# A 4 KB store of zeros into the output, issued behind the first loads

## Chip, cores, metric

One core of a Trainium2 chip. The time is device microseconds of one execution; the median of several is quoted. Kernels are compared only within the same rounds.

## The reference

A 3x3 convolution with padding 1, `x` of 16 x 64 x 64 x 64 and a weight of 128 x 64 x 3 x 3 in float32, nine tenths of the weight zero. The output is 16 x 128 x 64 x 64 in float32, 33.55 MB.

```
for b, co, ci, kh, kw:
    if weight[co, ci, kh, kw] != 0:
        output[b, co] += weight[co, ci, kh, kw] * x_pad[b, ci, kh:kh+h, kw:kw+w]
```

## The kernel before

Images are worked in eight pairs (64 channels of each image on one half of the partitions). GpSimd's queue loads x and casts it to bf16 on the way; SyncE's queue loads the weights and the head of the first pair in float32, and later stores the results, one image (2 MB) at a time, the last pair in four pieces of 1 MB. TensorE is kept warm with 27 matmuls on zeros until data is there.

```
    xs = [x_pool.tile([128, H, W], BF16, name=f"x{p}") for p in range(NP)]
    w_sb = const_pool.tile([C_OUT, C_IN * KH * KW], FP32, name="w_sb")
    nc.sync.dma_start(out=w_sb, in_=weight.rearrange("o i kh kw -> o (i kh kw)"))
    x_head = o_pool.tile([128, H, W], FP32, name="o")
    nc.sync.dma_start(out=x_head[:, 0:HEAD, :], in_=pair(0)[:, 0:HEAD, :])
    nc.gpsimd.dma_start(out=xs[0][:, HEAD:H, :], in_=pair(0)[:, HEAD:H, :])
    ...
    for p in range(1, NP):
        nc.gpsimd.dma_start(out=xs[p], in_=pair(p))

    idle_rhs = const_pool.tile([128, 128], BF16, name="idle_rhs")
    nc.vector.memset(idle_rhs, 0.0)
    idle_ps = psum_pool.tile([128, 128], FP32, name="ps")
    for _ in range(27):
        nc.tensor.matmul(idle_ps, idle_rhs, idle_rhs, start=True, stop=True)
    ... (weights cast and transposed, products, additions)
    for p in range(NP):
        o = [o_pool.tile([C_OUT, H, W], FP32, name="o") for _ in range(2)]
        last = p == NP - 1
        for blk in range(4):
            ... (16 rows of both images)
            if last and blk % 2 == 1:
                for n in range(2):
                    rows = slice(r0 - 16, r0 + 16)
                    nc.sync.dma_start(out=out[2 * p + n][:, rows, :], in_=o[n][:, rows, :])
        if not last:
            for n in range(2):
                nc.sync.dma_start(out=out[2 * p + n], in_=o[n])
```

Of the kernel before, what the change touches and what calls it, by code (L numbers as in the profile page):

```python
# [8 lines left out]
FP32 = mybir.dt.float32  # L9
# [18 lines left out]
def kernel(  # L28
# [6 lines left out]
    nc = tc.nc  # L35

    B, C_IN, H, W = x.shape
# [5 lines left out]
    const_pool = ctx.enter_context(tc.tile_pool(name="const", bufs=1))  # L43
# [25 lines left out]

    idle_rhs = const_pool.tile([128, 128], BF16, name="idle_rhs")  # L70
    nc.vector.memset(idle_rhs, 0.0)  # L71
    idle_ps = psum_pool.tile([128, 128], FP32, name="ps")
    for _ in range(27):
        nc.tensor.matmul(idle_ps, idle_rhs, idle_rhs, start=True, stop=True)  # L74
# [144 lines left out]
```

## Time and profile before

| | before |
|---|---|
| time, first 3 runs | 127.72 us (127.55 to 127.75) |
| span of the profiled run (which took 127.12 us, less than the three above) | 125.4 us |
| TensorE busy from / last addition ends | 7.12 / 111.76 us |
| first store issued / its first packet | 21.60 / 25.76 us |
| last landing that SyncE waits for | 124.2 us |

From the page of the kernel before: the busy tenths of the DMA engines in 40 slices, the packet counts, SyncE's queue (packets, MB, share of 16 engines' time), and the stores (KB each, median us from issue to landing).

```profile
DMA  5999999989999999999999999999999999999980
...
DMA packets 4044, 42.93 MB, mean 342 GB/s; under 512 B 448, under 2 KB 448, under 8 KB 704
...
q1 hardware_dynamic: 2880, 34.90, 66.2%
...
out_dram<-o SPq DMA_DIRECT2D x14, 2048.0 KB, 19.8
```

The DMA engines are full from the second slice nearly to the last, and a store of 2 MB takes 19.8 us to land, four times the 4.9 us that its bytes need at 428 GB/s. Stores queue up: the kernel is bound by DMA engine time, although TensorE is busy for most of the span too. (While x is loaded the rate is only some 220 GB/s with the engines just as full: the 7.86 MB that the page gives for GpSimd's queue are half of the 15.7 MB of float32 that it reads, so its bytes are counted after the cast.)

### The profile page before, as it was taken

The page shows a single profiled execution, that of the slowest core. Times are in us where ns is not written, and L with a number is a line of the kernel's source. Part 1 is how long each engine was busy: PE and PEld are TensorE (multiplying, and loading weights), DVE is VectorE, ACT ScalarE, POOL GpSimd, SP SyncE. Part 2 cuts the span into 40 slices and gives each one's busy share as a digit, 9 for nine tenths or more (in the row PEclk, how much of TensorE's full clock was granted, in tenths as well). Part 3 has the DMA queues.
Part 4 walks back from the last instruction along what each step waited for, and adds up shares of the span by engine and source line. Part 5 has one row for each costly group of instructions (what it writes and reads, how often), then busy time and mean ns, then how long its engine had stood idle before and what let it go on. Part 6 is the DMA issues. An engine that isn't in the chain of part 4 may idle for free.

```text
span 125.4 us, 2486 instructions
## 1 busy us (share of the span) xinstructions
PE 107.5 (86%) x1002; PEld 58.8 (47%) x1002; DVE 82.4 (66%) x135; ACT 39.0 (31%) x71; POOL 40.7 (32%) x45
## 2 busy tenths in 40 slices
PE   6679999999999999999999999999999999920000
PEld 6435555555555555555555555555555555500000
DVE  0463877877787778777877787778777877760000
ACT  4555323333333333333333333333333333300000
POOL 6936533333333333333333333333333300000000
PEclk9999999999999999999999999999999999997555
DMA  5999999989999999999999999999999999999980
GB/s 146 338 222 220 212 214 220 191 259 350 324 311 337 308 293 319 342 316 308 426 429 423 408 429 434 450 416 434 418 418 429 429 444 423 434 397 423 423 369 10
DMA packets 4044, 42.93 MB, mean 342 GB/s; under 512 B 448, under 2 KB 448, under 8 KB 704
## 3 DMA queue, kind: packets, MB, share of 16 engines
q1 hardware_dynamic: 2880, 34.90, 66.2%
q0 software_dynamic: 1152, 7.86, 30.7%
q8 instruction: 8, 0.13, 0.4%
q14 instruction: 4, 0.03, 0.1%
HBM read 17.07 MB, written 33.55 MB: 404 GB/s over the span
## 4 chain that ended last, share of the span: by engine, by line
PE 81%; DMA 4%; DVE 1%; issue 1%; DVEq 0%; SPq 0%
PE ps L135 81%; DMA o<-in_x_dram 4%; DVE o L168 1%; DVEq L214 0%; DVE x L87 0%; SPq L60 0%; DVEq L168 0%
## 5 line engine op out<-in xcount | busy, mean ns | idle before, releaser
L168 DVE TENSOR_TENSOR o<-ps,pc 128x512 f32<-128x512 f32 x124 | 77.8, 686 | 22.1 <-PE ps L135 19.8
L135 PE MATMUL ps<-x,wT 64*128 64x504 bf16 (+3 forms) x780 | 88.8, 373 | 1.5 <-DVE x L87 1.5
L135 PEld LDWEIGHTS <-wT 64*128 64x128 bf16 x966 | 55.2, 94 | 49.4 <-issue 1.5
L154 POOL TENSOR_TENSOR s<-x 128x512 bf16<-128x512 bf16 x31 | 35.6, 1152 | 57.7 <-PE ps L135 41.5
L161 ACT COPY pc<-ps 128x512 f32<-128x512 f32 x62 | 33.3, 589 | 64.0 <-issue 61.8
L135 PE MATMUL ps<-s,wT 64*128 64x512 bf16 (+1 forms) x186 | 25.7, 377 | 0.0
L74 PE MATMUL ps<-idle_rhs 128*128 128x128 bf16 x27 | 3.1, 310 | 1.0 <-DVE idle_rhs L71 1.0
L67 POOL DMA_DIRECT2D x<-in_x_dram x7 | 3.7, 561 | 0.0
L74 PEld LDWEIGHTS <-idle_rhs 128*128 128x128 bf16 x27 | 2.8, 144 | 1.0 <-DVE idle_rhs L71 1.0
L91 DVE CAST w_bf<-w_sb 128x192 bf16<-128x192 f32 (+1 forms) x4 | 1.3, 382 | 3.0 <-DMA w_sb<-in_weight_dram 3.0
L149 DVE COPY o<-ps 128x512 f32<-128x512 f32 x2 | 1.4, 692 | 2.0 <-PE ps L135 2.0
L148 ACT COPY o<-ps 128x512 f32<-128x512 f32 x2 | 1.2, 586 | 2.4 <-PE ps L135 2.4
L87 ACT CAST x<-o 128x576 bf16<-128x576 f32 (+1 forms) x2 | 1.5, 802 | 0.5 <-DMA o<-in_x_dram 0.5
L91 ACT ACT_TABLE_LOAD x1 | 1.3, 1283 | 0.7 <-PEq L203 0.7
L97 PE MATMUL ps<-ident,w_bf 128*128 128x128 bf16 x9 | 1.1, 292 | 0.4 <-DVE w_bf L91 0.4
L87 DVE CAST x<-o 128x576 bf16<-128x576 f32 x1 | 0.5, 460 | 1.4 <-DMA o<-in_x_dram 1.4
L91 ACT CAST w_bf<-w_sb 128x64 bf16<-128x64 f32 (+1 forms) x2 | 0.7, 418 | 1.9 <-DMA w_sb<-in_weight_dram 1.9
L97 PEld LDWEIGHTS <-w_bf 128*128 128x128 bf16 x9 | 0.8, 128 | 0.8 <-DVE w_bf L91 0.8
L101 DVE TENSOR_TENSOR wT<-ps,wT 128x384 bf16<-128x384 f32 x2 | 1.0, 550 | 0.0
L63 POOL DMA_DIRECT2D x<-in_x_dram x1 | 0.7, 696 | 0.8 <-POOLq L203 0.8
L71 DVE MEMSET idle_rhs<- 128x64 uint32 x1 | 0.1, 112 | 0.8 <-PEq L203 0.8
L110 ACT CAST wT<-ps 128x384 bf16<-128x384 f32 x1 | 0.5, 481 | 0.4 <-PE ps L97 0.4
(8 smaller groups left out, 1.9 us busy)
## 6 DMA issues: line engine op xcount, KB each, us to landing
out_dram<-o SPq DMA_DIRECT2D x14, 2048.0 KB, 19.8
x<-in_x_dram POOLq DMA_DIRECT2D x7, 1024.0 KB, 29.3
out_dram<-o SPq DMA_DIRECT2D x4, 1024.0 KB, 12.3
o<-in_x_dram SPq DMA_DIRECT2D x1, 1024.0 KB, 5.4
x<-in_x_dram POOLq DMA_DIRECT2D x1, 512.0 KB, 7.5
w_sb<-in_weight_dram SPq DMA_DIRECT2D x1, 288.0 KB, 3.1
```

Source lines behind the costliest of these rows:

```text
L67: nc.gpsimd.dma_start(out=xs[p], in_=pair(p))
L74: nc.tensor.matmul(idle_ps, idle_rhs, idle_rhs, start=True, stop=True)
L87: copy(out=xs[0][:, a:b, :], in_=x_head[:, a:b, :])
L91: copy(out=w_bf4[:, g, a:b, :], in_=w_v[:, k : k + b - a, :])
L97: nc.tensor.matmul(wps[:, j, :], src, ident, start=True, stop=True)
L101: nc.vector.tensor_tensor(out=wT[:, g], in0=wps, in1=wT[:, G1], op=SUB)
L135: nc.tensor.matmul(ps[n][:, lo:hi, c_lo:c_hi], tap(g, kw, n), src[q, a:b:step, c_lo + kw - 1 : c_hi + kw - 1], start=(i == 0), stop=(i == ...
L148: nc.scalar.copy(out=o[0][:, r0 : r0 + rows, :], in_=ps[0])
L149: nc.vector.tensor_copy(out=o[1][:, r0 : r0 + rows, :], in_=ps[1])
L154: nc.gpsimd.tensor_tensor(out=s, in0=xs[p][:, r0 : r0 + 16 : 2, :], in1=xs[p][:, r0 + 1 : r0 + 16 : 2, :], op=ADD)
L161: nc.scalar.copy(out=c, in_=shared[n])
L168: nc.vector.tensor_tensor(out=o[n][:, first : r0 + 16 : 2, :], in0=ps[n], in1=pc[n], op=ADD)
```

## The change

Each of the 16 DMA engines makes one small write to the output early, while compute waits for its first data. The intent isn't written down; the likely one is to have whatever the first write to the output costs out of the way before the real stores begin. The real store of image 0 overwrites the rows.

```
     nc.vector.memset(idle_rhs, 0.0)
+
+    zeros = const_pool.tile([16, W], FP32, name="zeros")
+    nc.vector.memset(zeros, 0.0)
+    nc.sync.dma_start(out=out[0, 0:16, 0, :], in_=zeros)
     idle_ps = psum_pool.tile([128, 128], FP32, name="ps")
```

## The prediction

> **What bounds the kernel now.** I read the chain of waits first, then distrusted it. It follows compute and ends with DVE:
>
> ```profile
> 1.17 5.41 DMA o<-in_x_dram
> ...
> 7.12 102.09 PE ps L135 x954
> ...
> 111.16 0.60 DVE o L168
> ```
>
> The columns are start in us, length in us, and what ran. TensorE is busy without a hole from 7.12 to 109.21, but the last addition is over at 111.76 and the span is 125.4 us. The chain says nothing of the last 13.6 us, in which only stores land. So the second view is what the store queue waited for:
>
> ```profile
> SPq L188 <- DVE o L168: 92.2, 14, 19.9
> SPq L214 <- DMA out_dram<-o: 11.6, 4, 4.4
> ```
>
> SyncE waits for results all through the kernel (92.2 us in 14 waits) and at the end for four landings (11.6 us). That the tail takes so long is a backlog of the DMA engines, and the third view, the run cut into stretches, shows it. The last two numbers of each line are the share of time the 16 DMA engines are busy and the GB/s they move:
>
> ```profile
> 2.00:3.00 1.00, 1.00 (x13) 1.00 (x11) 0.00 (x0) 0.02 (x1) 0.93 (x3) 1.00 1.11 345
> ...
> 7.00:20.00 13.00, 12.88 (x120) 6.83 (x121) 8.25 (x15) 5.52 (x10) 6.82 (x6) 1.00 1.04 217
> 20.00:22.00 2.00, 2.00 (x22) 1.14 (x20) 2.00 (x4) 0.54 (x2) 0.43 (x1) 1.00 1.09 229
> 22.00:23.00 1.00, 1.00 (x14) 0.57 (x10) 0.40 (x2) 0.54 (x2) 0.71 (x1) 1.00 0.96 197
> 23.00:24.00 1.00, 1.00 (x14) 0.50 (x10) 1.00 (x3) 0.00 (x0) 0.00 (x0) 1.00 1.17 213
> 24.00:25.00 1.00, 1.00 (x12) 0.53 (x10) 1.00 (x2) 0.37 (x1) 0.28 (x1) 1.00 1.25 164
> 25.00:26.00 1.00, 1.00 (x12) 0.56 (x10) 0.27 (x2) 0.70 (x2) 0.87 (x1) 1.00 0.73 156
> 26.00:62.00 36.00, 36.00 (x342) 19.28 (x339) 28.42 (x46) 11.83 (x22) 12.69 (x11) 1.00 1.02 326
> 62.00:110.00 48.00, 48.00 (x452) 25.67 (x450) 37.54 (x61) 16.12 (x30) 13.84 (x12) 1.00 1.01 428
> 110.00:121.00 11.00, 0.40 (x6) 0.00 (x0) 1.76 (x3) 0.00 (x0) 0.00 (x0) 0.71 1.00 421
> ```
>
> The engines are full from 2 us to 121 us (a packet is counted where it starts, hence shares over 1). The end is therefore set by DMA work: the start near 2 us, plus all bytes at the rate they go, plus the last landing. Compute only has to hand over stores before the backlog runs dry. How near that is: the 13th store is issued at 98.38, and the 12th (issued 86.17, 18.1 us to landing) lands at 104.3, so 5.9 us of slack at the tightest of the late places I worked out. A delay of TensorE of under some 5 us costs nothing in the end time; DMA engine time costs its full length.
>
> One oddity carries the uncertainty. At 22 to 26 us the rate falls below the 229 GB/s of the two microseconds before: missing are 32 + 16 + 65 + 73 = 186 GB/s over one microsecond each, that is 0.186 MB, or 0.81 us of the engines at 229 GB/s. In the single packets of the trace, loads of 8 KB that always take 0.624 us take 0.7 to 1.4 us between 23.4 and 26.6 us. The excess is 0.74 us per engine. The first store is issued just before, at 21.60, and its first packet starts at 25.76. No later store shows such a dip. I read it as a start-up cost of the first write to HBM, which is argued from timing only. The change looks meant for this: one small early write from each of the 16 engines.
>
> **What the Trainium skill says.** "DMA: Bandwidth & Descriptors", section "Why a DMA increments its semaphore by 16 and not by 1": the number of engines is the largest up to 16 that divides the slowest dimension, so 16 partitions give one row of 256 B per engine. The trace of before has no such transfer; it does have 128 data packets and 16 semaphore packets for each transfer (2880 packets on the hardware queue are 20 times 144). The same page, "Queues, rings and completion order": each engine takes one queue's descriptors in ring order. The trace agrees: the first packet of the head of x starts at 2.553 us, as the weights' last ones drain. The same page, "Specifications", has transfers under 512 B done as a read-modify-write; no packet of data that small is in this trace. "Trace Analysis", section "Roofline": a lone core is bounded by its 16 engines at about 435 GB/s in aggregate, not by its HBM share. The trace agrees, 428 GB/s from 62 to 110 us.
>
> **The change, part by part.** I compared the instruction order and semaphores of both builds. TensorE, ScalarE and GpSimd have the same instructions with the same waits.
>
> VectorE: one more memset of 64 words per partition, next to that of idle_rhs. That one has the same length per partition and took 0.112 us, ending at 0.93. The next VectorE work waits for the weights until 3.91, so 0.11 us goes into 2.97 us of idle. TensorE's warm-up waits only on the first memset. Nothing.
>
> SyncE: one more issue after the second load, whose 0.42 us ends at 1.59. Like its neighbours it takes 0.33 to 0.42 us and ends near 2.0; the next issue is at 21.60. Nothing.
>
> DMA work: per engine one data packet of 256 B and one semaphore packet. The trace gives semaphore packets 9 to 22 ns, and the smallest data packets, 2304 B, 93 ns typically. I take up to 0.09 us for the data, more than its bytes need, which leaves room for a read-modify-write. Sum: 0.01 + 0.09 = up to 0.1 us on a path that is full, so +0.05 to +0.1 us at the end. As bytes alone it would be 4 KB at 428 GB/s, 0.01 us.
>
> Where they fall: on the same ring behind the head of x, whose last data packet starts at 5.67 us. So the zeros move near 6 us and land near 7 to 8 us. The head's landing, which releases TensorE, isn't behind them.
>
> Waits: the first real store overwrites these rows and now waits for the zeros' landing too. That is done more than 10 us before its other waits end at 21.60, so it adds nothing. The semaphores of SyncE's DMAs rotate over eight; the extra DMA moves every store by one place, but a store that waits for a store still waits for the one eight before it. The renamed waits on VectorE mean the same.
>
> SBUF: 256 B more per partition, which shifts the later buffers. I expect nothing of it.
>
> Sum without the oddity: 127.72 + 0.1 = 127.8 us.
>
> **Rivals.** First, the start-up cost is paid by the zeros and is hidden, because a write of 256 B holds no large data back while loads keep streaming. Then the dip at 22 to 26 us goes, and the end comes 0.74 to 0.81 us earlier: about 127.0. For it: the dip occurs once, at the first write, and the new store touches each engine. Against it: in before the dip stretched packets of the loads, so whatever waits blocks them too.
>
> Second, the cost is paid once but not hidden: it moves to some time between 3 and 7 us, where the engines are just as full. The end stays, 127.7 to 127.8. It might push the landing of the head of x and so TensorE's start from 7.12 to as late as 7.9, which the slack of 5.9 us absorbs. A reader of the chain of waits alone would expect that to cost 0.8 us; I don't.
>
> Third, the cost is not tied to the first write but to large stores joining the loads, or to new addresses in the output. The zeros warm only 16 rows of the first image. Then the dip stays at 22 to 26 us: 127.7 to 127.8. If the zeros bring their own start-up cost besides, it is paid twice, 128.5.
>
> A fourth, that the new wait on the first store delays the stores, would need the zeros to land after 21.6 us. They would have to sit behind the loads' queue, which has its own ring, so I give it next to nothing.
>
> **Range and chances.** I give 55% to no net effect (127.7 to 127.8, rivals two and three), 30% to some or all of the gain (127.0 to 127.5), 15% to a second cost (up to 128.5). The three runs of before span 0.2 us. The middle of that is 127.6, with 126.9 to 128.2 for 8 in 10. 2% is 2.55 us; the largest cost or gain I can point at is 0.8 us, so both outer outcomes get 2%.
>
> **What would show it.** In the changed profile: the hardware queue has 2912 packets and 480 lie under 512 B (448 before); a 4 KB issue from zeros by SyncE starts near 1.6 us and lands 5 to 7 us later. The first real store is still issued near 21.6 us. TensorE's long stretch starts at 7.1 us (rival two: up to 7.9). The DMA share stays near 1.0 from 2 to 121 us, and the last semaphore comes within 0.2 us of 124.2. The rate between 22 and 26 us tells the rivals apart: near 229 GB/s and more if the cost has moved or gone, still near 160 if it hasn't; a dip near 3 to 7 us that before lacks would be the moved cost. The prediction is wrong if the first store is issued more than 1 us later, if the engines fall idle in mid-run, or if TensorE gets a second hole.

## The result and the profile after

127.72 us median (127.57 to 127.94, 4 runs) against 127.63 us (127.35 to 127.75, 4 runs) for the kernel before. The ratio is 1.0011 with a 95% interval of 0.9989 to 1.0034: the same. (Ratios are the mean time of one kernel's runs over that of the other's of the same rounds, so not quite the ratio of the medians quoted. Executions over 1.5% slower than the fastest of the same kernel are left out of the means.)

The page of the changed kernel, the same rows and the new issue:

```profile
DMA  4999999999999999999999999999999999999980
...
DMA packets 4076, 42.93 MB, mean 341 GB/s; under 512 B 480, under 2 KB 480, under 8 KB 736
...
q1 hardware_dynamic: 2912, 34.90, 66.0%
...
out_dram<-zeros SPq DMA_DIRECT2D x1, 4.0 KB, 6.0
```

32 packets more, 16 of data and 16 of semaphores, and one issue that lands 6.0 us later, as predicted. In the single packets the data ones last 31 ns each and start at 6.05 to 6.96 us.

SyncE's issues in order of time (start, length), before and after:

```profile
21.60 77.77 SPq L188 DMA_DIRECT2D out_dram<-o  x14
104.73 7.66 SPq L185 DMA_DIRECT2D out_dram<-o  x4
```

```profile
1.65 0.42 SPq L75 DMA_DIRECT2D out_dram<-zeros  x1
23.70 77.72 SPq L192 DMA_DIRECT2D out_dram<-o  x14
106.84 8.08 SPq L189 DMA_DIRECT2D out_dram<-o  x4
```

Here is something that the prediction said would not happen: in this run every real store is issued 2.1 us later. The chain of waits of the changed kernel says where that began,

```profile
1.18 5.82 DMA o<-in_x_dram
...
7.54 103.77 PE ps L139 x954
```

and the stretches of one microsecond show the rest. The column before the DMA share is TensorE's granted clock:

```profile
8.00:9.00 1.00, 1.00 (x12) 0.57 (x10) 0.88 (x2) 0.54 (x1) 0.38 (x1) 0.82 1.16 238
9.00:10.00 1.00, 1.00 (x8) 0.41 (x6) 0.00 (x0) 0.00 (x0) 1.00 (x2) 0.50 0.94 197
10.00:11.00 1.00, 1.00 (x7) 0.36 (x4) 0.58 (x1) 0.58 (x1) 1.00 (x2) 0.50 1.13 238
11.00:12.00 1.00, 1.00 (x8) 0.51 (x6) 0.11 (x1) 0.00 (x0) 0.98 (x1) 0.50 1.05 221
```

The head of x landed 0.41 us later, TensorE started 0.42 us later, and then its clock was at half for 3.4 us (8.6 to 12.0 us in the clock records; 7 or 8 matmuls per microsecond in place of 12 to 14). TensorE's stretch took 103.77 us instead of 102.09, so everything behind it is 2.1 us late. The end is late by less: the last landing is at 124.7 us and was at 124.2, and the two profiled runs, of 127.57 and 127.12 us, differ by as much. What SyncE waited for at the end, after:

```profile
SPq L218 <- DMA out_dram<-o: 9.5, 4, 2.4
```

Before it was 11.6 us. The wait for the last landings shrank by the 2.1 us by which compute slipped: the backlog of the DMA engines took up the late work.

Last, the slow-down of the loads ahead of the first real store, which the zeros might have removed. The changed kernel, by microsecond (DMA share and GB/s last):

```profile
24.00:25.00 1.00, 1.00 (x14) 0.57 (x12) 0.40 (x2) 0.64 (x2) 0.82 (x1) 1.00 1.18 246
25.00:26.00 1.00, 1.00 (x12) 0.55 (x10) 1.00 (x2) 0.00 (x0) 0.00 (x0) 1.00 1.21 213
26.00:27.00 1.00, 1.00 (x14) 0.53 (x10) 1.00 (x3) 0.27 (x1) 0.18 (x1) 1.00 1.00 131
27.00:28.00 1.00, 1.00 (x12) 0.49 (x10) 0.32 (x1) 0.80 (x2) 0.98 (x1) 1.00 0.84 131
```

It is all there, 2.1 us later along with the store: 131 GB/s for two microseconds. The stretching of the loads' packets sums to 0.88 us per engine (0.74 before). So the zeros did not pay for it. Three questions were put to the chip: is the end really set by DMA time; was the late start the doing of the zeros; and what is the slow-down tied to?

### The profile page after: what moved, and what is told of

The parts are those of the page before. It is cut to its first block, busy times and chain, and to the rows that moved or that the text cites. A ratio compares the mean times of both kernels' runs of the same rounds, so it can differ in the third digit from the quotient of the medians.

```text
span 125.8 us, 2488 instructions
## 1 busy us (share of the span) xinstructions
PE 109.2 (87%) x1002; PEld 58.9 (47%) x1002; DVE 82.3 (65%) x136; ACT 39.0 (31%) x71; POOL 40.7 (32%) x45
## 4 chain that ended last, share of the span: by engine, by line
PE 82%; DMA 5%; DVE 1%; issue 1%; DVEq 0%; SPq 0%
PE ps L139 82%; DMA o<-in_x_dram 5%; DVE o L172 1%; DVEq L218 0%; DVE x L91 0%; SPq L60 0%; DVEq L172 0%
## 5 line engine op out<-in xcount | busy, mean ns | idle before, releaser
L139 PE MATMUL ps<-x,wT 64*128 64x504 bf16 (+3 forms) x780 | 90.5, 379 | 2.2 <-DVE x L91 2.2
```

The lines of the kernel that those rows point to most:

```text
L139: nc.tensor.matmul(ps[n][:, lo:hi, c_lo:c_hi], tap(g, kw, n), src[q, a:b:step, c_lo + kw - 1 : c_hi + kw - 1], start=(i == 0), stop=(i == ...
```

## Experiments

Every result was right but for one. "Excess" below is what the 8 KB loads of GpSimd's queue took over their usual 0.624 us, summed over the stretch and divided by 16 engines, from the single packets of the trace. Single loads of 0.80 to 0.87 us that lie elsewhere, a few in each profile, are not counted.

### The kernel before against itself

No edit.

> The kernel before against itself: what the comparison can resolve, and how much the start-up varies from profile to profile. All theories expect a ratio of 1.000 with an interval of about 0.2% on either side. It settles a side question: in the changed kernel's profile the head of x landed 0.41 us later than before and TensorE's clock was at half from 8.6 to 12.0 us. If that is run-to-run variation, this second profile of an unchanged kernel may show another landing than 6.59 us; if the zeros caused it, it lands at 6.6 us again (within 0.1) with no half-clock stretch.

127.63 us (127.31 to 130.51), ratio 0.9987 (0.9972 to 1.0003); the run of 130.51 us counts as slow and is left out. So a comparison resolves 0.2% at best, and a kernel compared with itself came out at 0.9987. In this second profile of an unchanged kernel the head of x landed at 6.85 us, not 6.59, and TensorE started at 7.39. So 0.26 of the 0.41 us come and go without any change. The clock did not drop in this profile.

### The changed kernel again

No edit.

> The changed kernel once more, five rounds. My theory (the end is set by DMA engine time; the zeros add 0.05 us per engine, one packet of 31 ns and one semaphore packet of 22 ns): ratio 1.000 to 1.001. Rival, that the zeros hold up the head of x and with it something at the end: ratio 1.003 or more, the head again landing at 7.0 us. The slow-down of the loads ahead of the first real store is to be there again, about 0.8 us of excess per engine.

127.68 us against 127.64, ratio 0.9989 (0.997 to 1.0008): no cost, and the rival's 1.003 is excluded. The head landed at 6.80 us, earlier than in the repeat of the kernel before, and with eight such stores (next run) at 6.76 us. The zeros do not hold it up. The clock was again at half for one stretch of 3.4 us, and the excess at the first store was 1.06 us per engine. The excess counts 8 KB loads only, and none of them runs yet when the zeros pass near 6 us. The loads that do, of 4 KB (usually 0.324 us), took at most 0.44 us next to the zeros in the changed kernel and 0.35 in this repeat, against 0.39 in the kernel before.

### Eight stores of zeros

```
-    nc.sync.dma_start(out=out[0, 0:16, 0, :], in_=zeros)
+    for b in range(8):
+        nc.sync.dma_start(out=out[b, 0:16, 0, :], in_=zeros)
```

> Eight such stores of zeros, into the first 16 channels of images 0 to 7. My theory: eight times 0.053 us per engine, 0.4 us at the end, ratio 1.003 against before, and the slow-down at the first real store stays, about 0.8 us per engine. Rival, a first-touch cost for each image or region of the output, which one image could not show: with eight images touched the slow-down shrinks or goes, and the ratio is 0.995 to 0.998. Second rival, the small stores cost a fixed time each on a chain (issue 0.42 us and landing about 1 us or more, one after the other): 3 us or more at the end, ratio 1.02.

127.78 us, ratio 1.0007 (0.9992 to 1.0022). The excess stays, 0.97 us per engine, so touching more images does not help. The issues fill SyncE's queue from 1.65 to 7.1 us and nobody waits for it. My sum was too high: 0.4 us was expected, 0.1 us measured, and the interval ends at 0.28 us. The packet lengths of SyncE's and GpSimd's queues, summed and divided by 16 engines, did rise by 0.4 us, from 121.78 in the repeat of the changed kernel to 122.17 here. But the records of packets overlap (the DMA share is 1.04 from 7 to 20 us in the kernel before). That a few short packets hide in part beside the loads is my reading, no run shows it.

### A large early store

```
     nc.vector.memset(idle_rhs, 0.0)
+    nc.sync.dma_start(
+        out=out[0][:, 0:9, :].rearrange("c h w -> c (h w)"), in_=w_sb)
```

> The early store is large: the 288 KB of the loaded weights go into rows 0 to 8 of image 0 (right in the end, since the real store overwrites them), issued near 4 us in place of the zeros. Both theories pay its engine time, 0.295 MB at 428 GB/s, 0.7 us. If the slow-down at the first real store is a one-off of the first sizeable write, it moves to 4 to 8 us and is gone at 22 to 26 us; the time is then 0.7 us over before, ratio 1.005. If it belongs to the large stores joining the stream of loads, it stays at the first real store (0.7 to 0.9 us excess per engine), with the same ratio of 1.005. If it moves and is hidden, ratio 1.000.

128.46 us, ratio 1.0049 (1.0033 to 1.0065). The profiled run took 301.5 us and is of no use for the stores: TensorE's matmuls lasted 823 ns each (373 usually), and its clock records are empty. It counts as slow and is left out of the ratio; what slowed it is not known. It was repeated:

> The early store of 288 KB once more, because the profiled run of the first was one of 301 us, in which [...]the loads were over before the first large store; its packets went out at 7.5 to 13.0 us with no load stretched near them. If the slow-down belongs to the first sizeable write, none is left at the first real store near 22 to 28 us; if it belongs to the large stores joining the loads, 0.7 to 1.0 us of excess per engine are there again. Time in both cases 0.6 us over before (measured once, ratio 1.0049).

128.05 us, ratio 1.0027 (1.0015 to 1.0039). The early packets (2304 B) pass at 7.0 to 12.4 us with no 8 KB load over 0.63 us, and the excess at the first real store is there, 0.46 us. A write of 288 KB does not pay for the slow-down in advance. The cost measured twice, 0.3 and 0.6 us, is near or under the 0.7 us of its bytes.

### The zeros late

```
+            if p == 0 and blk == 1:
+                nc.vector.memset(zeros, 0.0)
+                nc.sync.dma_start(out=out[0, 0:16, 0, :], in_=zeros)
```

(in place of the early ones, in the loop over blocks)

> The same 4 KB of zeros, issued by SyncE after the second block of the first pair, near 16 us, when its DMA queue has been idle for 10 us and the loads stream alone. If the slow-down of the loads comes from a queue that starts again after idling, or from the first write during the load stream, it appears ahead of the zeros' packets (16 to 20 us) and not at the first real store. If it belongs to the first large store, it stays there, 0.7 to 0.9 us of excess per engine just before the first 16 KB packet, and the zeros pass with packets of 31 ns and no load above 0.7 us near them. Time within 0.3% of before in both cases.

127.75 us, ratio 0.999 (0.9968 to 1.0012). The zeros were issued at 19.13 us and their packets went at 22.57 to 23.14. By microsecond, around them and around the first real store:

```profile
22.00:23.00 1.00, 1.00 (x14) 0.47 (x10) 0.28 (x1) 0.77 (x2) 0.94 (x1) 1.00 0.97 199
23.00:24.00 1.00, 1.00 (x14) 0.53 (x12) 0.99 (x2) 0.00 (x0) 0.00 (x0) 1.00 1.04 215
...
27.00:28.00 1.00, 1.00 (x14) 0.45 (x11) 1.00 (x3) 0.00 (x0) 0.00 (x0) 1.00 1.31 188
28.00:29.00 1.00, 1.00 (x12) 0.52 (x10) 0.61 (x2) 0.99 (x2) 0.90 (x1) 1.00 0.82 147
```

The first write of the whole execution passes in the middle of the loads without slowing them (no load of 21 to 24 us over 0.625 us), and the slow-down still comes at the first large store, 0.69 us per engine. It is neither the first write nor a queue that wakes up.

This profile shows one thing more. TensorE began at 7.55 us and until 13.6 us started a pair of matmuls every 0.43 us instead of 0.22, so the first real store was issued at 24.98 us, 3.4 us later than before. This execution took 128.00 us, the longest of its four, but within what the kernel before took in the same rounds (127.65 to 128.16). (The trace has no clock record before 13.58 us; where there is none, the view's clock column shows 1.00, so the pace of the matmuls is the better sign.)

### A large load in the place of a store

```
+            if p == 0 and blk == 1:
+                extra = o_pool.tile([128, H, W], FP32, name="o")
+                nc.vector.memset(extra[:, 0:1, :], 0.0)
+                nc.sync.dma_start(out=extra[:, 0:HEAD, :], in_=pair(0)[:, 0:HEAD, :])
```

(on the kernel before)

> On the kernel before, SyncE issues near 16 us a second load of the 1 MB head of x into a buffer that nothing reads, in packets of 8 KB. Engine time 1.05 MB at 428 GB/s: 2.4 us at the end, ratio 1.019, if DMA engine time sets the end; none if it doesn't. If the slow-down comes from large packets of SyncE's queue joining the other queue's stream, whatever their direction, it appears ahead of this load's first packet (0.7 us excess or so) and may be gone at the first store. If it belongs to writing to HBM, it stays at the first store alone.

129.68 us, ratio 1.014 (1.0119 to 1.0161): 1.8 us more, of 2.4 expected. DMA time that runs fully beside busy TensorE comes out at the end, though not all of it; where the other 0.6 us went I didn't find. The load was issued at 17.55, its first packet went at 20.97 us, 3.4 us later, and no other load near it took over 0.63 us. At the first store the excess is 0.59 us. So the long way from issue to first packet is not the slow-down (it is there without it), and large packets coming into SyncE's queue are not enough: it takes stores.

### Compute late

```
-    for _ in range(27):
+    for _ in range(80):
```

(on the kernel before)

> On the kernel before, 80 warm-up matmuls in place of 27: compute starts late. 53 more at 0.06 to 0.11 us push TensorE's start from 7.1 us to about 9 to 11 us, and its end and the issue of all stores with it by 2 to 4 us. My theory, that DMA engine time sets the end and compute has at least 5.9 us of slack: within 0.3 us of before, ratio 0.998 to 1.002. Rival, the chain of waits as the page gives it (TensorE 81%): the end moves by the same 2 to 4 us, ratio 1.016 to 1.03.

127.36 us against 127.78, ratio 0.9965 (0.9941 to 0.9988). The chain of waits of this kernel:

```profile
0.99 7.29 PE ps L74 x80
...
9.01 102.10 PE ps L135 x954
```

TensorE starts 1.9 us later than before, with its clock never at half in that stretch, and the first store is issued at 23.51 us. The end does not move by any of it. The chain that gives TensorE 81% of the span names an engine that has slack. That it should come out faster I had not foreseen, so it was repeated:

> The late compute start once more, five rounds: it came out 0.35% faster than before (ratio 0.9965, interval 0.9941 to 0.9988), which no theory of mine foresaw. If that was chance, the ratio is 0.999 to 1.001 here; if a later first store or the warm clock helps, it is 0.9965 again.

127.54 us, ratio 0.9983 (0.997 to 0.9996). Half of the first gain, with TensorE starting at 8.03 us in this profile; still under 1, but hardly lower than the kernel before against itself (0.9987). If there is a gain, it is of 0.2 to 0.3%, and its cause is open.

### The last store left out

```
-                for n in range(2):
+                for n in range(2 if blk == 1 else 1):
```

(on the kernel before, last pair; the result is wrong)

> On the kernel before, the very last store of 1 MB is left out, so the result is wrong on purpose in rows 32 to 63 of the last image; all compute stays. My theory: the engines save 1.05 MB at 428 GB/s, 2.4 us, ratio 0.981. Rival, compute plus a fixed landing time sets the end: the last issue comes 0.6 us earlier, so at most 0.6 us less, ratio 0.995.

125.25 us against 127.78, ratio 0.9804 (0.9758 to 0.9849). The compute is all there, and in this profile it was late as well:

```profile
7.37 103.77 PE ps L135 x954
```

The time falls by 2.5 us with the bytes, 2.4 expected. (The record calls the verdict unclear, as the interval reaches to both sides of 2%; the rival's 0.995 lies outside it.) TensorE's stretch is 103.77 us long, as in the changed kernel, with the clock at half from 8.4 to 11.8 us. This kernel has no zeros, nor has the one with the extra load, which shows the same. So the half-clock stretch does not need the zeros.

### An early piece of the first result

```
+            if p == 0 and blk == 0:
+                nc.sync.dma_start(out=out[0][:, 0:16, :], in_=o[0][:, 0:16, :])
...
-                nc.sync.dma_start(out=out[2 * p + n], in_=o[n])
+                a = 16 if p == 0 and n == 0 else 0
+                nc.sync.dma_start(out=out[2 * p + n][:, a:H, :], in_=o[n][:, a:H, :])
```

(on the kernel before)

> On the kernel before, rows 0 to 15 of image 0 are stored as soon as they are done, near 12 us, in packets of 4 KB (512 KB); the other rows follow at the old time. SyncE's queue then runs, falls idle and starts again. If the slow-down is a one-off of the first store of results, it lies ahead of this early one and is gone at 22 to 28 us. If it comes each time that stores join the loads, it is there twice. If it needs 16 KB or 12 KB packets, it stays at the second alone. As the bytes are the same and the engines are full, the time stays within 0.3% of before.

127.34 us against 127.76, ratio 0.9973 (0.9958 to 0.9989). The early store of 512 KB was issued at 13.67 us, its 4 KB packets ran from 17.09 to 23.2 us, and the next store's began at 26.91:

```profile
16.00:17.00 1.00, 1.00 (x14) 0.49 (x10) 1.00 (x3) 0.06 (x1) 0.00 (x0) 1.00 1.15 205
17.00:18.00 1.00, 1.00 (x12) 0.53 (x10) 0.59 (x1) 1.00 (x2) 0.91 (x1) 1.00 0.79 164
...
26.00:27.00 1.00, 1.00 (x14) 0.49 (x10) 1.00 (x2) 0.45 (x1) 0.35 (x1) 1.00 1.23 217
27.00:28.00 1.00, 1.00 (x12) 0.53 (x10) 0.27 (x2) 0.63 (x2) 0.80 (x1) 1.00 0.84 258
```

The loads are stretched twice (packets over 0.7 us counted): 35 packets of up to 0.86 us ahead of the first piece (excess 0.37 us per engine) and 27 of up to 1.00 us ahead of the second (0.33 us). It is no one-off. It came both times when a store of results joined the loads after SyncE's queue had run empty.

### Both small gains together

The edits of the last one and the 80 warm-up matmuls.

> The two edits that came out slightly faster than before, together: the early store of rows 0 to 15 (ratio 0.9973) and 80 warm-up matmuls (0.9965 and 0.9983). If both gains are real and independent they add up, ratio 0.994 to 0.996; if both are the same small thing or mostly chance, 0.997 to 0.999. The loads are to be stretched at two places again, before the 4 KB packets and before the 12 KB packets.

127.30 us (127.15 to 127.41) against 127.72, ratio 0.9964 (0.9949 to 0.9979), hardly more than the early piece alone. The excess is 0.29 and 0.22 us in the two places. It is faster than the kernel before by 0.4%. The interval leaves out 1, but it just overlaps that of the kernel before against itself (0.9972 to 1.0003), so the gain is small and not beyond doubt. The changed kernel was not in these rounds.

The excess, in one table (us per engine):

| kernel | store or load that joins | packets | excess | longest load |
|---|---|---|---|---|
| before | first store | 16 KB | 0.74 | 1.40 |
| after | first store | 16 KB | 0.88 | 1.39 |
| zeros late | zeros | 256 B | 0.00 | 0.63 |
| zeros late | first store | 16 KB | 0.69 | 1.34 |
| extra load | load | 8 KB | 0.00 | 0.63 |
| extra load | first store | 16 KB | 0.59 | 1.29 |
| large early store, repeat | early store | 2304 B | 0.00 | 0.63 |
| large early store, repeat | first store | 16 KB | 0.46 | 1.22 |
| early piece | early piece | 4 KB | 0.37 | 0.86 |
| early piece | second store | 12 KB | 0.33 | 1.00 |

The longest single stretch grows with the size of the store's packets (0.86 to 0.88 us at 4 KB, 0.96 to 1.00 at 12 KB, 1.22 to 1.64 at 16 KB, over all fast profiles). That would fit a load that shares its engine with a store packet which has no record of its own yet; it is an argument, no run shows it.

## Why the prediction was right, point by point

**DMA time sets the end.** Right, and shown from both sides: 1 MB of stores less is 2.5 us less, 1 MB of loads more is 1.8 us more, and a compute start 1.9 us later costs nothing. "DMA engine time costs its full length" was too strong: of added work 1.8 of 2.4 us, 0.3 and 0.6 of 0.7, and 0.1 of 0.4 came out at the end.

**The slack of compute.** Right so far as it was used: in the changed kernel's own profile compute was 2.1 us late and the wait at the end was 2.1 us shorter. The largest slip is that of the late zeros, 3.4 us, in an execution of 128.00 us, no longer than some of the kernel before. The full 5.9 us were not tried, and they look too many: they run from the 13th issue to the 12th landing, which comes when the slowest engine is done. With the slip of 3.4 us the DMA share already fell to 0.73 and 0.81 at 101 to 103 us (0.92 and 1.08 in the kernel before), so some engines seem to have waited for work.

**The zeros' own cost.** Right in size, a bit high. 31 ns for the data packet where up to 90 ns were allowed. That is three times the 10 ns of its bytes at the pace of the 2304 B packets (93 ns); whether the read-modify-write that the skill has for such sizes is part of it, no run shows. The term that was mis-sized is the claim that packet times add up on the full path: eight stores cost 0.1 us, not 0.4.

**No cost on engines and waits.** Right: issue at 1.65 us, landing 6.0 us later, 16 us ahead of the one store that waits for it. "So the zeros move near 6 us and land near 7 to 8 us" holds as well.

**The slow-down at the first store.** The step "I read it as a start-up cost of the first write to HBM" was wrong. The zeros, early or late, are the first write and cause none, and stores after an idle spell cause it again. Its size, "0.81 us of the engines", was reckoned from the 229 GB/s of two microseconds; from the 217 GB/s of 7 to 20 us the same sum gives 0.64. The third rival, "to large stores joining the loads", is what the runs support; packets of 2304 B and less did not cause it, and a load of 8 KB packets did not either. Why it comes, and how much of it reaches the end, stays open. As the rivals all lay within 0.8 us, the wrong reading did not harm the forecast; that it held in spite of it is no merit of the reading.

**What would show it wrong.** One of the signs was badly chosen: "the first store is issued more than 1 us later" came true, by 2.1 us, and meant nothing. It contradicted the text's own slack. Two more signs failed: the last landing came at 124.7 us, not within 0.2 us of 124.2, and the rate at 22 to 26 us (213, 197, 246 and 213 GB/s) would have said that the dip was gone, where it had only moved with the store. Of the 2.1 us, 0.42 are TensorE's later start, and 1.68 come with TensorE's clock at half for 3.4 us after its gap before the first product, seen in kernels without the zeros as well. The Trainium skill describes it, in "TensorE: Matmul & The Clock Gate", section "Part 1: The HAM clock gate (the "warmup" mystery)": a free-running window of about 3.4 us decides the clock, so the same kernel may or may not be caught. The traces agree: the half-clock stretches on record are 3.41 us long, and the length of the gap does not decide it alone: gaps of 1.93 us (the repeat of before) and 2.23 us (the repeat of the large early store) went free, gaps of 1.98 us (eight stores of zeros) and 2.17 us (the changed kernel) did not. What parts them is when the clock had risen: in the three profiles in which it rose at 5.34 to 5.70 us it stayed up, in the six in which it rose at 3.88 to 5.22 us it fell 3.41 us later. That is a pattern of nine profiles, not a test. Only the 80 warm-up matmuls close the gap, to 0.24 us.

## What to carry to other kernels

When the DMA engines are full from start to end, judge a change by the DMA time it adds or removes, whatever the chain of waits names; compute that slips by 2 us inside the backlog costs nothing. A few tiny transfers are then nearly free, and they warm nothing unless some run shows a cost that was paid once. Before believing in a first-time cost, make the event happen twice and see whether the cost does.

## What the Trainium skill lacked or had wrong

- "DMA: Bandwidth & Descriptors" has nothing on loads slowing down when large stores join them on the same engines: 8 KB loads of 0.624 us took up to 1.6 us, 0.5 to 1.1 us per engine in all, where 16 KB stores began.
- The same page has transfers under 512 B as read-modify-write and off line rate. A 256 B store packet lasted 31 ns in the records, three times the 10 ns of its bytes at the pace of the 2304 B packets, so it was off line rate here too. What the page doesn't say is what a few of them cost beside running loads: 128 cost 0.1 us at the end.
- The same page gives about 0.6 us to the first byte on SyncE's path, without saying for what load of the engines. From the start of the issue it was 1.0 us for the weights, when the engines were empty (0.74 to 1.75 us). While loads filled the engines it was 3.4 us for a load and for zeros (17.55 to 20.97 and 19.13 to 22.57), and 4.2 us for the first store (21.60 to 25.76).
- "TensorE: Matmul & The Clock Gate" warns of a clock stuck low for 50 us and more. Whether the execution of 301.5 us was such a case stays open: a pair of its matmuls started every 0.62 us (0.43 where the clock was at half), it has no clock record, and some of its warm-up matmuls start 55 ns apart, as the last of the 80 do (55 to 56 ns, clock record at full).
